# Differences of prepared weight blocks on GpSimd in place of VectorE, in an encoder kernel

## The chip, the cores and the metric

One core of a Trainium2 chip runs the whole program. The metric is the device time of one execution in microseconds (us); of several runs the median counts.

The engines go by their short names in the profile: PE is TensorE (matmuls; PEld is its loading of the stationary operand), DVE is VectorE, ACT is ScalarE, POOL is GpSimd, and SP is the engine whose queue issues most of the DMAs.

## The reference

Two layers of a bidirectional encoder on x of 256 tokens by 1024 features, in float32:

```python
for l in range(DEPTH):                                     # DEPTH = 2
    x = x + 0.5 * swiglu(rms_norm(x, ffn1_norm[l]), ffn1_w_gate[l], ffn1_w_up[l], ffn1_w_down[l])
    h = rms_norm(x, mix_norm[l])
    ...                                                    # two kinds of attention on h, gated and merged
    x = x + merged @ w_out[l]
    x = x + 0.5 * swiglu(rms_norm(x, ffn2_norm[l]), ffn2_w_gate[l], ffn2_w_up[l], ffn2_w_down[l])

def swiglu(x, w_gate, w_up, w_down):
    return (jax.nn.silu(x @ w_gate) * (x @ w_up)) @ w_down  # 1024 -> 2816 -> 1024
```

There are thus four feed-forward stages, and the change touches nothing else.

## The kernel before

**Split operands.** Every matmul is made three times with split operands: a value is taken apart into a rounded part (high, made by ScalarE at line 190) and the rest (low, made by VectorE at line 191 as value minus high), and the products high by high, high by low and low by high are added up (lines 174 to 176). So each tile of weights is loaded from memory into one of four `raw` buffers (128 x 1024 values, `RAW = 4`), then ScalarE writes `wh` and VectorE writes `wl`, each in a ring of six, and TensorE uses both. The raw buffer is free once `wl` is written.

**Gate and up.** A feed-forward stage works through 11 chunks of 256 hidden features. A chunk loads four tiles of gate and up weights and makes 48 matmuls of 128 x 512, 24 for each of the two tiles of tokens, into one of two PSUM banks `g`. `glu` then makes `hh` from a bank: ScalarE applies silu to the gate half (line 463), VectorE multiplies by the up half (line 464). When that is done, the bank is free for the chunk after. `send` passes `hh` to a DMA transpose (ScalarE line 332, SP line 335). `arrive`, a chunk or so later, puts the transposed result together in a buffer `a` (ScalarE line 344), makes four sums and differences of its 128 x 128 blocks (VectorE, line 351) and splits it into `hi` and `lo`.

**Down.** The down projection takes the hidden features in pairs of blocks. For a chunk marked F or G in `PLAN = "SFGFGGFGGSS"`, its 2 x 2 blocks of weights are multiplied with the 2 x 2 blocks of hidden values by seven products in place of eight. This needs differences of weight blocks, which `differences` makes: two of 128 x 512 into a tile `u`, two into a tile `v` that build on those of `u`. `u` and `v` are then split like weights. `u`, `v` and the buffer `a` of `arrive` share two buffers (the tag `sums`), so a `v` waits until the `a` of its chunk has been split.

**Preparation.** Of the eight such pairs in a stage, three have their differences made early, during gate and up, where `prepare` keeps the split parts (`uh`, `ul`, `vh`, `vl`) until the down projection. `PREP = {3: 1, 5: 3, 7: 6}` says at which gate-and-up chunk the pair of which chunk is prepared; the first stage of all has `PREP_FIRST = {5: 1, 7: 3, 8: 6}`. A preparation loads two rows of blocks into raw buffers, which it holds until the last difference that reads them. The other five pairs have theirs made in the down projection, by `sevens`.

**Order.** TensorE runs in the order of the code. A scheduler orders the instructions of the other engines by its own estimate of their times, and each engine then runs its queue strictly in that order.

Of the kernel before, what the change touches and what calls it, by code (L numbers as in the profile page):

```python
# [17 lines left out]
ALU = mybir.AluOpType  # L18
# [40 lines left out]
def hybrid_encoder(ctx, tc, x, w_gu1, w_d1, w_in, b_gate, qk_gain, rpb, sink, t5,  # L59
                   w_bna, w_bsw, w_out, w_gu2, w_d2, c_mask, c_band, out):  # L60
    nc = tc.nc
# [127 lines left out]
    def split_to(hi, lo, src):  # L189
        last_hi[0] = linked("act", lambda: nc.scalar.activation(hi, src, AF.Copy))  # L190
        linked("dve", lambda: nc.vector.tensor_tensor(lo, src, hi.bitcast(F32), ALU.subtract))  # L191
# [126 lines left out]
    def ffn(l, n, w_gu, w_d, after):  # L318
        with tc.tile_pool(name="ffn", bufs=1) as fp:
# [40 lines left out]
            stored = {}  # L360

            def block_row(k, c0=0, n=2):
                r = ring.tile([P, 2, 512], F32, name="raw", tag="raw", bufs=RAW)[:, :n, :]
                nc.sync.dma_start(r, w_d[l, k * P:(k + 1) * P, :n * 512].rearrange("p (h n) -> p h n", h=n))
                return r

            def differences(r0, r1, into):
                sub = lambda to, x, y: nc.vector.tensor_tensor(to, x, y, ALU.subtract)  # L368
                u = fp.tile([P, 2, 512], F32, name="u", tag="sums", bufs=2)
                sub(u[:, 0, :], r1[:, 1, :], r0[:, 1, :])  # L370
                sub(u[:, 1, :], r0[:, 1, :], r0[:, 0, :])
                us = into("u", u)
                v = fp.tile([P, 2, 512], F32, name="v", tag="sums", bufs=2)
                sub(v[:, 0, :], r1[:, 1, :], u[:, 1, :])
                sub(v[:, 1, :], r1[:, 0, :], v[:, 0, :])
                return us, into("v", v)

            def prepare(c):
                def into(name, r):
                    hl = [fp.tile([P, 2, 512], F32R, name=f"{name}{p}{c}", tag=f"{name}{p}{c}") for p in "hl"]  # L380
                    split_to(*hl, r)
                    return hl
                stored[c] = differences(block_row(2 * c), block_row(2 * c + 1), into)

            def sevens(c):
                r0 = block_row(2 * c, n=1 if c in stored else 2)
                r1 = block_row(2 * c + 1)
                place = ("xh0", "xl0", "xh1", "xl1")[(c - PLAN[:c].count("S")) % 4]
                both = act.tile([P, 2, 512], F32R, name="corner", tag=place)
                corner = [both[:, i, :] for i in range(2)]  # L390
                split_to(*corner, r0[:, 0, :])
                low = parts(r1)
                us, vs = stored.get(c) or differences(r0, r1, lambda name, r: parts(r))
                if on_way and c >= 5:
                    arrive()
                half = lambda pair, i: [p[:, i, :] for p in pair]
                return (("1", 0, corner), ("2", 1, half(low, 0)), ("3", 6, half(low, 1)), ("5", 3, half(us, 1)),
                        ("6", 4, half(vs, 0)), ("4", 2, half(vs, 1)), ("7", 5, half(us, 0)))
# [67 lines left out]
            for c in range(NFC):  # L466
                first = n == 0 and c == 0
                pair = [None]
                if first:
                    both, second = opening(w_gu, l, lambda ps: glu(0, ps, pair))  # L470
                elif n == 0 and c == 1:
                    pieces = second
                else:
                    pieces = columns(w_gu, l, c * 512, 512)
                if c >= 2:
                    arrive()
                prep = PREP if n else PREP_FIRST
                if c in prep:
                    prepare(prep[c])
                for t in range(T):  # L480
                    if not first:
                        glu(t, project(t, pieces, 512), pair)
                    elif t:
                        glu(t, both[t], pair)
                send(c, pair[0])
# [376 lines left out]
```

## Time and profile before

| | |
|---|---|
| median of three runs | 1064.51 us (1064.47 to 1069.99) |
| profiled execution | 1065.35 us; the span from first to last instruction is 1063.6 us |
| TensorE, VectorE, ScalarE, GpSimd busy | 1051.7, 879.6, 746.6, 117.7 us |
| granted TensorE clock | 1.00 of full speed over the span |
| DMA | 224.15 MB, the queue of SP busy 72.4% of 16 engines' span |

Rows of the timeline give the start in us from the span's start, the duration in us, the engine, the line, the operation, the tile written and those read, the shapes, and at the end, in brackets, how long the engine had been idle and what ended that. "Waits" give the waiting engine and its line, an arrow, who ended the wait, and then total us, times and longest us. TensorE's matmuls overlap: one of 128 x 512 shows about 0.39 us, and the next starts before it ends, so the step from start to start is what counts. Rows by source line give the shortest, median and longest duration in ns.

### The profile page before, as it was taken

How to read it: one execution, taken by the hardware profiler on the slowest of the kernel's cores; microseconds unless marked ns; L12 is line 12 of the kernel's file. 1: busy time of each engine (PE TensorE's matmuls, PEld its weight loads, DVE VectorE, ACT ScalarE, POOL GpSimd, SP SyncE). 2: the span in 40 equal slices, each digit the busy share in tenths (PEclk: the TensorE clock that was granted, in tenths of full speed). 3: DMA queues.
4: the chain of work that ended last, by engine and by line, in shares of the span. 5: the costliest groups of instructions: out<-in, count | busy, mean ns of one | idle time of the engine just before them, and what ended most of it. 6: DMA issues, size and time to landing. Idle time of an engine off the chain costs nothing.

```text
span 1063.6 us, 14462 instructions
## 1 busy us (share of the span) xinstructions
PE 1051.7 (99%) x4949; PEld 870.7 (82%) x4949; DVE 879.6 (83%) x1337; ACT 746.6 (70%) x1070; POOL 117.7 (11%) x118
## 2 busy tenths in 40 slices
PE   8999999999999999999999999999999999999998
PEld 6888787888888888888788888878888888878886
DVE  6678899889886858879977887998898866788797
ACT  6777775788773667786567886757887646678772
POOL 1000130243420000000000000004534100000000
PEclk9999999999999999999999999999999999999999
DMA  7989875765654589996758998757566546799862
GB/s 246 263 220 268 253 207 191 222 197 154 195 181 155 170 234 253 248 252 196 224 174 226 262 259 213 215 160 247 175 195 179 190 156 192 215 256 245 240 203 98
DMA packets 145291, 224.15 MB, mean 211 GB/s; under 512 B 54033, under 2 KB 60209, under 8 KB 145217
## 3 DMA queue, kind: packets, MB, share of 16 engines
q1 hardware_dynamic: 145024, 223.14, 72.4%
q8 instruction: 39, 0.64, 0.3%
q14 instruction: 36, 0.29, 0.1%
q0 software_dynamic: 192, 0.08, 0.1%
HBM read 210.59 MB, written 1.06 MB: 199 GB/s over the span
## 4 chain that ended last, share of the span: by engine, by line
PE 55%; DVE 16%; DMA 16%; ACT 7%; issue 4%; SPq 0%; ACTq 0%; DVEq 0%
PE g L174 12%; PE g L176 12%; PE g L175 12%; DMA raw<-in_w_gu 10%; DVE wl L191 8%; DMA raw<-in_w_d 4%; PE acc L174 3%; PE acc L176 3%; PE acc L175 3%; ACT a L344 3%; ACT wh L190 2%; ACT lo L332 2%; DVE v L368 2%; PE sc L585 1%; PE po L620 1%
## 5 line engine op out<-in xcount | busy, mean ns | idle before, releaser
L191 DVE TENSOR_TENSOR wl<-raw,wh 128x1024 fp32r<-128x1024 f32 x336 | 405.4, 1219 | 63.5 <-ACT wh L190 60.7
L190 ACT ACTIVATE wh<-raw 128x1024 fp32r<-128x1024 f32 x336 | 345.2, 1042 | 99.8 <-DMA raw<-in_w_gu 44.9
L174 PE MATMUL g<-wh,xh 128*128 128x512 f32 (+1 forms) x976 | 382.5, 392 | 0.8 <-DVE hh L464 0.3
L175 PE MATMUL g<-wl,xh 128*128 128x512 f32 (+1 forms) x976 | 377.5, 387 | 0.4 <-DVE wl L191 0.4
L176 PE MATMUL g<-wh,xl 128*128 128x512 f32 (+1 forms) x976 | 377.4, 387 | 0.0
L176 PEld LDWEIGHTS g<-wh,xl 128*128 128x128 f32 x976 | 183.4, 188 | 38.5 <-DVE xl L191 0.6
L174 PEld LDWEIGHTS g<-wh,xh 128*128 128x128 f32 x976 | 183.5, 188 | 38.2 <-DVE hh L464 4.8
L175 PEld LDWEIGHTS g<-wl,xh 128*128 128x128 f32 x976 | 183.6, 188 | 34.4 <-DVE wl L191 1.4
L175 PE MATMUL acc<-wl,hi 128*128 128x512 f32 x180 | 70.2, 390 | 0.9 <-DVE wl L191 0.9
L174 PE MATMUL acc<-wh,hi 128*128 128x512 f32 x180 | 70.7, 393 | 0.0
L176 PE MATMUL acc<-wh,lo 128*128 128x512 f32 x180 | 70.1, 390 | 0.0
L180 POOL TENSOR_TENSOR rs_y<-ms,mhalf 128x1 f32<-128x1 f32 x12 | 7.7, 645 | 547.0 <-DVE ms L228 538.3
L344 ACT ACTIVATE a<-hi 128x1024 uint16<-128x1024 uint16 x44 | 59.5, 1353 | 0.0
L332 ACT ACTIVATE lo<-hh 128x1024 uint16<-128x1024 uint16 x44 | 46.2, 1051 | 18.4 <-DVE hh L464 18.3
L464 DVE SCALAR_TENSOR_TENSOR hh<-g,rs_y,hh 128x256 f32<-128x256 f32 x88 | 42.1, 479 | 18.0 <-ACT hh L463 18.0
L351 DVE TENSOR_TENSOR a<-a 128x128 f32<-128x128 f32 x128 | 32.0, 287 | 28.9 <-ACT a L344 28.1
L463 ACT ACTIVATE hh<-g,rs_y 128x256 f32<-128x256 f32 x88 | 40.4, 459 | 19.4 <-PE g L176 19.0
L368 DVE TENSOR_TENSOR u<-raw 128x512 f32<-128x512 f32 x64 | 42.2, 690 | 13.1 <-DMA raw<-in_w_d 12.8
L191 DVE TENSOR_TENSOR lo<-a,hi 128x896 fp32r<-128x896 f32 (+1 forms) x44 | 43.0, 977 | 11.1 <-ACT hi L190 11.1
L598 POOL TENSOR_TENSOR S<-S,sm 128x512 f32<-128x512 f32 x32 | 37.2, 1161 | 65.5 <-DVE sm L597 38.2
L190 ACT ACTIVATE hi<-a 128x896 fp32r<-128x896 f32 (+1 forms) x44 | 37.7, 856 | 8.6 <-DVE a L351 8.0
L190 ACT ACTIVATE corner<-raw 128x512 fp32r<-128x512 f32 x32 | 20.0, 626 | 30.8 <-DMA raw<-in_w_d 27.6
(186 smaller groups left out, 1506.3 us busy)
## 6 DMA issues: line engine op xcount, KB each, us to landing
raw<-in_w_gu SPq DMA_DIRECT2D x176, 512.0 KB, 4.6
raw<-in_w_d SPq DMA_DIRECT2D x100, 512.0 KB, 4.4
raw<-in_w_in SPq DMA_DIRECT2D x64, 512.0 KB, 4.6
raw<-in_w_out SPq DMA_DIRECT2D x16, 512.0 KB, 3.5
bb<-in_b_gate SPq DMA_DIRECT2D x16, 256.0 KB, 3.5
raw<-in_w_bsw SPq DMA_DIRECT2D x8, 512.0 KB, 3.9
raw<-in_w_bna SPq DMA_DIRECT2D x8, 512.0 KB, 3.6
raw<-in_w_d SPq DMA_DIRECT2D x12, 256.0 KB, 2.6
```

Source lines behind the costliest of these rows:

```text
L174: nc.tensor.matmul(ps, xh, wh, start=first, stop=False)
L175: nc.tensor.matmul(ps, xh, wl, start=False, stop=False)
L176: nc.tensor.matmul(ps, xl, wh, start=False, stop=last)
L190: last_hi[0] = linked("act", lambda: nc.scalar.activation(hi, src, AF.Copy))
L191: linked("dve", lambda: nc.vector.tensor_tensor(lo, src, hi.bitcast(F32), ALU.subtract))
L332: apart[c] = nc.scalar.activation(z.rearrange("p (two n) -> p two n", two=2), hh.bitcast(U16).rearrange("p s (n two) -> p two (s n)", two= ...
L344: joined = nc.scalar.activation(a[:, :4, :].bitcast(U16).rearrange("p s (n two) -> p two (s n)", two=2), zT.rearrange("p (two s) n -> p tw ...
L351: nc.vector.tensor_tensor(a[:, to, :], a[:, x, :], a[:, y, :], op)
L368: sub = lambda to, x, y: nc.vector.tensor_tensor(to, x, y, ALU.subtract)
L463: linked("act", lambda: nc.scalar.activation(h, gate, AF.Silu, scale=rstd[t]))
L464: linked("dve", lambda: nc.vector.scalar_tensor_tensor(h, up, rstd[t], h, op0=ALU.mult, op1=ALU.mult))
L598: nc.gpsimd.tensor_tensor(S_, S_, sm.unsqueeze(2).to_broadcast([P, T, S]), ALU.mult)
```

## The change

`differences` gets the engine that subtracts as an argument. `prepare`, the caller in gate and up, passes GpSimd; `sevens`, the caller in the down projection, passes nothing and stays on VectorE.

```diff
-            def differences(r0, r1, into):
-                sub = lambda to, x, y: nc.vector.tensor_tensor(to, x, y, ALU.subtract)
+            def differences(r0, r1, into, engine=nc.vector):
+                sub = lambda to, x, y: engine.tensor_tensor(to, x, y, ALU.subtract)
                 u = fp.tile([P, 2, 512], F32, name="u", tag="sums", bufs=2)
                 sub(u[:, 0, :], r1[:, 1, :], r0[:, 1, :])
                 sub(u[:, 1, :], r0[:, 1, :], r0[:, 0, :])
...
-                stored[c] = differences(block_row(2 * c), block_row(2 * c + 1), into)
+                stored[c] = differences(block_row(2 * c), block_row(2 * c + 1), into, nc.gpsimd)
```

The scheduler's order moves with it. On VectorE, at the second preparation of a stage with `PREP` (here the second stage, chunk 5), this is the piece up to the product hh of that chunk's first tile of tokens:

```order
 L464 SCALAR_TENSOR_TENSOR hh<-g,rs_y,hh 128x2x128
-L368 TENSOR_TENSOR u<-raw 128x512 x2
-L351 TENSOR_TENSOR a<-a 128x128 x4
-L191 TENSOR_TENSOR wl<-raw,wh 128x1024
+L351 TENSOR_TENSOR a<-a 128x128 x4
+L191 TENSOR_TENSOR wl<-raw,wh 128x1024 x2
 L191 TENSOR_TENSOR ul_4203<-u,uh_4202 128x1024
-L191 TENSOR_TENSOR wl<-raw,wh 128x1024
 L191 TENSOR_TENSOR lo_4188<-a,hi_4187 128x896
 L464 SCALAR_TENSOR_TENSOR hh<-g,rs_y,hh 128x256
```

The two differences u are gone from VectorE, and the second split of weights now stands ahead of the split of u instead of behind it. The next piece is what follows there, up to the split of v:

```order
 L464 SCALAR_TENSOR_TENSOR hh<-g,rs_y,hh 128x256
-L191 TENSOR_TENSOR wl<-raw,wh 128x1024
-L368 TENSOR_TENSOR v<-raw,u 128x512
-L191 TENSOR_TENSOR wl<-raw,wh 128x1024
-L368 TENSOR_TENSOR v<-raw,v 128x512
-L191 TENSOR_TENSOR wl<-raw,wh 128x1024
+L191 TENSOR_TENSOR wl<-raw,wh 128x1024 x3
 L464 SCALAR_TENSOR_TENSOR hh<-g,rs_y,hh 128x2x128
 L191 TENSOR_TENSOR vl_4210<-v,vh_4209 128x1024
```

The two differences v no longer stand between the three splits of weights. On ScalarE, at the same preparation, between the copies of send and arrive (lo, a) and the chunk's silu (hh):

```order
 L332 ACTIVATE lo_4157<-hh 128x1024
 L344 ACTIVATE a<-hi_4066 128x2x512
-L190 ACTIVATE wh<-raw 128x1024
+L190 ACTIVATE wh<-raw 128x1024 x2
 L190 ACTIVATE uh_4202<-u 128x1024
-L190 ACTIVATE wh<-raw 128x1024
 L190 ACTIVATE hi_4187<-a 128x896
 L463 ACTIVATE hh<-g,rs_y 128x256
```

The high part of u moved behind the second split of weights. On GpSimd, the twelve differences of the first stage go between the load of the small bias table and the load of the vector that the bias of the second kind of attention is made in:

```order
 L496 DMA table<-in_t 8x32
+L368 TENSOR_TENSOR u<-raw 128x512 x2
+L368 TENSOR_TENSOR v<-raw,u 128x512
+L368 TENSOR_TENSOR v<-raw,v 128x512
+L368 TENSOR_TENSOR u<-raw 128x512 x2
+L368 TENSOR_TENSOR v<-raw,u 128x512
+L368 TENSOR_TENSOR v<-raw,v 128x512
+L368 TENSOR_TENSOR u<-raw 128x512 x2
+L368 TENSOR_TENSOR v<-raw,u 128x512
+L368 TENSOR_TENSOR v<-raw,v 128x512
 L495 DMA vec<-in_c_band 8x511
```

Nothing else in GpSimd's queue stands among them. SP's queue keeps its order but for the end of the first stage's gate and up, where a transpose moved by two loads.

## The prediction

> **What bounds the kernel now.** I read the busy shares first, then the waits of TensorE, then the instructions that the diff touches, then the timeline of one preparation.
>
> ```profile
> PE 1051.7 (99%) x4949; PEld 870.7 (82%) x4949; DVE 879.6 (83%) x1337; ACT 746.6 (70%) x1070; POOL 117.7 (11%) x118
> PE g L175 <- DVE wl L191: 0.4, 1, 0.4
> PE g L174 <- DVE hh L464: 0.3, 2, 0.2
> PEld g L174 <- DVE hh L464: 4.8, 11, 0.6
> PEld g L175 <- DVE wl L191: 1.4, 3, 0.9
> PEld acc L175 <- DVE wl L191: 1.3, 1, 1.3
> ```
>
> The first line is the busy time of the engines; the others are who waited for whom: total us, times, longest. TensorE (PE) is the bound. It waits on VectorE (DVE) for two things: the gated product hh, whose end frees a PSUM bank, and the low parts wl of the split weights. All of that is 4.8 + 1.4 + 1.3 = 7.5 us of idle weight loading at most, and 0.4 + 0.3 us of idle matmul in gate and up. That is the ceiling of any gain from relieving VectorE.
>
> What moves, and what GpSimd (POOL) needs for the same shape, stands in the rows by source line (ns min/median/max):
>
> ```profile
> L368 DVE TENSOR_TENSOR u<-raw x64: 676/685/959, 65.9 to 1039.9; 128x512 f32<-128x512 f32 x64
> L368 DVE TENSOR_TENSOR v<-raw,u x32: 677/685/694, 75.5 to 1040.6; 128x512 f32<-128x512 f32 x32
> L598 POOL TENSOR_TENSOR S<-S,sm x32: 1041/1042/1880, 226.8 to 831.1; 128x512 f32<-128x512 f32 x32
> L692 POOL TENSOR_TENSOR b<-t,mask x16: 1184/1194/2062, 240.5 to 818.6; 128x512 f32<-128x512 f32 x16
> L191 DVE TENSOR_TENSOR wl<-raw,wh x336: 683/1220/1987, 7.3 to 1048.4; 128x1024 fp32r<-128x1024 f32 x164, 128x512 fp32r<-128x512 f32 x4
> ```
>
> The maxima of the last three rows are worth following. The timeline of GpSimd (two rows) and VectorE (two rows) in the attention stage shows them:
>
> ```profile
> 247.06 1.04 POOL L598 TENSOR_TENSOR S<-S,sm 128x512 f32<-128x512 f32 x1 [2.22 <-PE g L176]
> 252.20 1.85 POOL L598 TENSOR_TENSOR S<-S,sm 128x512 f32<-128x512 f32 x1 [4.10 <-PE pt L606]
> 247.20 1.99 DVE L191 TENSOR_TENSOR wl<-raw,wh 128x1024 fp32r<-128x1024 f32 x1
> 251.95 1.20 DVE L191 TENSOR_TENSOR wl<-raw,wh 128x1024 fp32r<-128x1024 f32 x1
> ```
>
> At 247 GpSimd is first: the split that starts 0.14 us behind it takes 1.99 us in place of 1.22, 0.77 longer. At 251.95 VectorE is first, and GpSimd's operation takes 1.85 us in place of 1.04, 0.81 longer. So the two exclude each other, whoever comes first, when both read two tensors from SBUF; of GpSimd's 1.04 us, 0.14 + 0.77 = 0.91 are closed to VectorE. In gate and up nearly every VectorE instruction is of that kind.
>
> **The change part by part.** *Off VectorE:* 12 preparations (three in each of four feed-forward stages) of four differences, 48 x 0.685 = 32.9 us of its 879.6. *Onto GpSimd:* 48 operations. Their price on GpSimd is not in the trace; the two rows above bound it at 1.04 and 1.19 us. I take 1.04, since that operation, too, runs through plain rows of 512 and the other reads an overlapping pattern. *The lock:* if VectorE has work throughout, each costs it 0.91 and saves 0.685, that is 4 x 0.225 = 0.9 us more per preparation; if VectorE was idle, it saves up to 2.7. The answer lies in the windows, so here is the second preparation of the second feed-forward stage, VectorE first, then ScalarE (ACT), then the first matmul of the next chunk:
>
> ```profile
> 416.69 1.29 DVE L368 TENSOR_TENSOR u<-raw 128x512 f32<-128x512 f32 x2 [0.98 <-DMA raw<-in_w_d]
> 418.10 1.02 DVE L351 TENSOR_TENSOR a<-a 128x128 f32<-128x128 f32 x4
> 419.04 1.22 DVE L191 TENSOR_TENSOR wl<-raw,wh 128x1024 fp32r<-128x1024 f32 x1
> 420.17 1.22 DVE L191 TENSOR_TENSOR ul<-u,uh 128x1024 fp32r<-128x1024 f32 x1
> 421.31 1.22 DVE L191 TENSOR_TENSOR wl<-raw,wh 128x1024 fp32r<-128x1024 f32 x1
> 422.44 1.09 DVE L191 TENSOR_TENSOR lo<-a,hi 128x896 fp32r<-128x896 f32 x1
> 423.44 0.48 DVE L464 SCALAR_TENSOR_TENSOR hh<-g,rs_y,hh 128x256 f32<-128x256 f32 x1
> 424.33 1.23 DVE L191 TENSOR_TENSOR wl<-raw,wh 128x1024 fp32r<-128x1024 f32 x1 [0.41 <-ACT wh L190]
> 425.47 0.69 DVE L368 TENSOR_TENSOR v<-raw,u 128x512 f32<-128x512 f32 x1
> 426.19 1.23 DVE L191 TENSOR_TENSOR wl<-raw,wh 128x1024 fp32r<-128x1024 f32 x1
> 427.33 0.69 DVE L368 TENSOR_TENSOR v<-raw,v 128x512 f32<-128x512 f32 x1
> 427.99 1.23 DVE L191 TENSOR_TENSOR wl<-raw,wh 128x1024 fp32r<-128x1024 f32 x1
> 416.71 1.36 ACT L344 ACTIVATE a<-hi 128x1024 uint16<-128x1024 uint16 x1
> 418.87 1.04 ACT L190 ACTIVATE uh<-u 128x1024 fp32r<-128x1024 f32 x1
> 419.81 1.05 ACT L190 ACTIVATE wh<-raw 128x1024 fp32r<-128x1024 f32 x1
> 420.76 0.95 ACT L190 ACTIVATE hi<-a 128x896 fp32r<-128x896 f32 x1
> 424.44 0.39 PE L174 MATMUL g<-wh,xh 128*128 128x512 f32 x1
> ```
>
> *The u part.* Both u wait for their rows from memory until 416.69, on any engine. GpSimd then runs them 416.69 to 417.73 and 417.73 to 418.77. The four small a are ready when ScalarE's a ends, 416.71 + 1.36 = 418.07, and meet the second u's lock: they start at about 418.65 to 418.77 in place of 418.10, so +0.6. VectorE saved nothing by losing the u, as it then only waits. Behind them the order is a, wl, wl, ul, lo, hh without a gap, so hh is 0.6 late as well. ScalarE's order adds a second reason: uh now stands behind the second wh, so hi starts after uh. That wh ran at 419.81 without an idle row, so its weights had landed by then; hi starts between 420.76 and 0.94 later. At the late end lo starts at 423.1 in place of 422.44, +0.7, no more than the lock alone. I take 0.65.
>
> *The v part.* The first v waits for lo, in whose buffer it writes. It is therefore ready when VectorE reaches hh and is ahead of the next wl, where before it stood behind it. Lo ends 0.65 late at 424.2, v holds the lock until 425.1 or 425.2, and that wl starts there in place of 424.33: +0.8. It ends at 426.4, the second v goes next until 427.4, the second wl starts there in place of 426.19: +1.2. The third wl then starts at about 428.6 in place of 427.99: +0.6. So the weights' low parts come 0.6 to 1.2 late, and the raw buffers behind them are reloaded so much later.
>
> A preparation by itself thus costs 0.6 to 1.2 us of lateness, with GpSimd at 1.19 some 0.3 more; where VectorE would have been idle at every lock it costs 0. I take 1.0.
>
> *What covers it.* How long TensorE can do without hh is read at the start of the next chunk, here for the first and third preparation of the same stage (hh, then the matmul that needs its bank; in the third also the two matmuls ahead of it):
>
> ```profile
> 400.73 0.48 DVE L464 SCALAR_TENSOR_TENSOR hh<-g,rs_y,hh 128x256 f32<-128x256 f32 x1
> 402.68 0.39 PE L174 MATMUL g<-wh,xh 128*128 128x512 f32 x1
> 445.96 0.48 DVE L464 SCALAR_TENSOR_TENSOR hh<-g,rs_y,hh 128x256 f32<-128x256 f32 x1
> 445.78 0.39 PE L175 MATMUL g<-wl,xh 128*128 128x512 f32 x1
> 446.01 0.39 PE L176 MATMUL g<-wh,xl 128*128 128x512 f32 x1
> 446.49 0.50 PE L174 MATMUL g<-wh,xh 128*128 128x512 f32 x1
> ```
>
> The cover is 402.68 - 401.21 = 1.47 us in the first preparation and 424.44 - 423.92 = 0.52 in the second. In the third there is none: hh ends at 446.44 and the matmul starts at 446.49, 0.48 behind its predecessor, where the step ahead of it was 0.23. So the cover shrinks by about 1 us per preparation already: loads, ScalarE and VectorE around it are a chain that is slower than TensorE there, and lateness is carried on to the next one.
>
> *The sum.* First preparation: 1.0 late, covered by 1.47, carried on. Second: 0.65 of its own u part plus 1.0 carried, less 0.52, is 1.1 us of stall. Third: about 0.35 from the second's v part and 0.65 to 1.2 of its own, uncovered: 1.0 to 1.5, I take 1.3. That is 2.4 us per stage and 9.6 for four. The first stage prepares at chunks 5, 7 and 8 in place of 3, 5 and 7; I take it as like the others. With lateness 0.6 and nothing carried it is 0.1 + 0.6 = 0.7 per stage, 3 in all; with 1.5 and all carried 4.5 - 0.5 = 4 per stage, 16 in all.
>
> The profiled execution took 1065.35 us, 0.84 above the median of 1064.51. 1065.35 + 9.6 = 1074.95, and by the median 1074.1: I say 1074.
>
> *What costs nothing.* GpSimd has room: beside 117.7 us it gets 48 x 1.04 to 1.19, 50 to 57 us, none of it beside attention. The one queue piece behind the new operations, the bias vector at line 495, waits for ScalarE in any case and is first read in attention. SP issues in the same order in three stages; two of its loads per preparation now wait for GpSimd's last reading of a raw row instead of VectorE's, at 418.77 and 427.4 in place of 417.98 and 428.02: 0.8 late once, 0.6 early once, and in the sum with the lateness above.
>
> The Trainium skill has the exclusion as a rule ("SBUF — State Buffer", section "Who interferes with whom"): the shared port pair is an exclusive lock held for the whole instruction, and the other fully blocks. The 1.99 and 1.85 us above bear that out within 0.13 us; by the rule's letter each lock closes 1.04 and not 0.91, and as an estimate every preparation would be some 0.2 later, 2.4 us in all, which makes 1076.5.
>
> **The rivals.** *Not slower: the locks fall into idle time.* VectorE idles 0.98 ahead of u and 0.41 ahead of the first wl in the window, and it loses 2.74 us of work per preparation. If a preparation comes no more than 0.5 late and the chain makes that up before the next, only the uncovered third one stalls: 4 x 0 to 0.5 us on 1064.5, so 1064 to 1067. For it: the first preparation has 1.47 us of cover, and a chunk without one lies between. Against it: that chunk does not restore the cover today. It decides where lateness per preparation is under 0.5.
>
> *Faster: VectorE's relief counts.* Then the waits for hh and wl shrink: at most 7.5 us, 1057; half of it, 1061. Against it: VectorE's second half of every preparation is exchanged for a lock of at least the same length. The skill's "Perfetto Trace Analysis", section "Optimizing Scalar/DVE Operations", says that with a saturated VectorE moving work to GpSimd may make sense, and in the same place that the shared read port may make it useless; the 1.99 us row speaks for the second half.
>
> *Much slower: GpSimd lags.* If a difference takes 1.2 and waits out a split of 1.22 each time, the chain u, u, v, v takes 4 x 2.4 = 9.7 us beside a window of about 15; raw rows are held longer, and if that doubles the lateness, 2 x 9.6 = 19 us make 1084. Against it: at 247 the lock was GpSimd's as soon as it came free.
>
> **How the numbers follow.** Forecast 0.60 (1067 to 1081), not slower 0.27, faster 0.06, much slower 0.07. About 0.5%, 5.3 us, is what a measurement tells from no change here. Slower: 0.55 of the forecast and the much slower, 0.62. Same: the rest of the forecast, the not slower, half of the faster: 0.35. Faster: 0.03. The range from 1063 to 1081 leaves out the much slower and most of the faster.
>
> **What would show it.** GpSimd busy at 170 us or more, with differences of 1.04 to 1.2 and some near 1.9; splits near 1.9 in gate and up; VectorE's busy time down by clearly less than 32.9; waits of TensorE for hh at the second and third preparations, together near 10 us in place of 4.8. Wrong if hh still ends ahead of its matmul there, or if the waits for wl grow and those for hh do not.

## The result, and the profile after

The changed kernel took 1076.63 us (median of 6 runs, 1074.41 to 1079.14), the kernel before, beside it, 1068.67 (median of 6, 1064.47 to 1069.99). The ratio is 1.0084, 95% interval 1.0066 to 1.0101: slower, by 8 to 9 us. The median of 1064.51 that stood at the start was that of three runs, two of them at the low end of what later runs show. The profiled execution of the changed kernel took 1077.21 us, its span is 1075.4.

The rows below are the busy times on the page, then the waits of TensorE, then the rows by source line of the moved differences and of the split (ns min/median/max), and the group of all splits of weights (busy us, mean ns).

```profile
PE 1055.4 (98%) x4949; PEld 870.4 (81%) x4949; DVE 879.2 (82%) x1289; ACT 746.9 (69%) x1070; POOL 196.1 (18%) x166
PEld g L174 <- DVE hh L464: 16.0, 17, 2.3
PE g L174 <- DVE hh L464: 8.5, 8, 1.9
PEld g L175 <- DVE wl L191: 5.2, 10, 2.1
L368 POOL TENSOR_TENSOR u<-raw x24: 1288/1299/2280, 62.7 to 975.7; 128x512 f32<-128x512 f32 x24
L368 POOL TENSOR_TENSOR v<-raw,u x12: 1280/1287/1294, 75.0 to 983.4; 128x512 f32<-128x512 f32 x12
L368 POOL TENSOR_TENSOR v<-raw,v x12: 2149/2154/2162, 76.4 to 984.8; 128x512 f32<-128x512 f32 x12
L191 DVE TENSOR_TENSOR wl<-raw,wh x336: 680/1220/2367, 7.4 to 1060.3; 128x1024 fp32r<-128x1024 f32 x164, 128x512 fp32r<-128x512 f32 x4
L191 DVE TENSOR_TENSOR wl<-raw,wh 128x1024 fp32r<-128x1024 f32 x336 | 430.2, 1297 | 65.6 <-ACT wh L190 63.0
```

VectorE lost 48 instructions, 32.9 us of work, and is as busy as before: 879.2 us against 879.6. What was taken off came back mostly as longer splits, 430.2 us now; of before the same group's row is

```profile
L191 DVE TENSOR_TENSOR wl<-raw,wh 128x1024 fp32r<-128x1024 f32 x336 | 405.4, 1219 | 63.5 <-ACT wh L190 60.7
```

A difference takes GpSimd 1.29 us, and the second v of every preparation takes 2.15, since it waits for a split to end. TensorE's waits for hh went from 4.8 to 16.0 us.

The second preparation of the second feed-forward stage, to be read beside the window in the prediction: GpSimd, VectorE, ScalarE, then the next chunk's first matmul.

```profile
419.85 2.55 POOL L368 TENSOR_TENSOR u<-raw 128x512 f32<-128x512 f32 x2 [10.35 <-DMA raw<-in_w_d]
429.60 1.29 POOL L368 TENSOR_TENSOR v<-raw,u 128x512 f32<-128x512 f32 x1 [7.20 <-DVE lo L191]
430.97 2.15 POOL L368 TENSOR_TENSOR v<-raw,v 128x512 f32<-128x512 f32 x1
422.77 1.02 DVE L351 TENSOR_TENSOR a<-a 128x128 f32<-128x128 f32 x4 [2.40 <-ACT a L344]
426.09 1.23 DVE L191 TENSOR_TENSOR wl<-raw,wh 128x1024 fp32r<-128x1024 f32 x1 [1.16 <-ACT wh L190]
429.37 0.48 DVE L464 SCALAR_TENSOR_TENSOR hh<-g,rs_y,hh 128x256 f32<-128x256 f32 x1
429.87 5.46 DVE L191 TENSOR_TENSOR wl<-raw,wh 128x1024 fp32r<-128x1024 f32 x3
425.00 1.06 ACT L190 ACTIVATE wh<-raw 128x1024 fp32r<-128x1024 f32 x1 [1.36 <-DMA raw<-in_w_gu]
425.97 1.04 ACT L190 ACTIVATE uh<-u 128x1024 fp32r<-128x1024 f32 x1
429.90 0.50 PE L174 MATMUL g<-wh,xh 128*128 128x512 f32 x1 [1.11 <-DVE hh L464]
454.32 0.50 PE L174 MATMUL g<-wh,xh 128*128 128x512 f32 x1 [1.91 <-DVE hh L464]
```

Both u run from 419.85 to 422.40, for the most part while VectorE is idle (its hh before ends at 420.38): its four a wait 2.40 us for ScalarE and start at 422.77. No lock touches them. ScalarE waits 1.36 us for the weights of the second wh, and only then comes uh, then hi, lo and hh. Behind hh both v hold VectorE: three splits take 5.46 us, where three without a lock take 2 x 1.14 + 1.23 = 3.51. But VectorE's own two v, 0.69 us each, no longer stand between them: the last of the three ends 5.96 us behind the start of hh, against 5.78 in the window of before. TensorE waits 1.11 us for hh here and 1.91 at the third preparation.

So two things stood side by side: the lock, and an order on ScalarE that the scheduler chose along with it. The experiments take them apart.

### The profile page after: what moved, and what is told of

Same layout as the page of the kernel before. It is cut to its first block, busy times and chain, and to the rows that moved or that the text cites. A ratio compares the mean times of both kernels' runs of the same rounds, so it can differ in the third digit from the quotient of the medians.

```text
span 1075.4 us, 14504 instructions
## 1 busy us (share of the span) xinstructions
PE 1055.4 (98%) x4949; PEld 870.4 (81%) x4949; DVE 879.2 (82%) x1289; ACT 746.9 (69%) x1070; POOL 196.1 (18%) x166
## 4 chain that ended last, share of the span: by engine, by line
PE 54%; DVE 19%; DMA 13%; ACT 8%; issue 5%; POOL 1%; ACTq 0%; DVEq 0%; POOLq 0%
PE g L174 12%; PE g L176 12%; PE g L175 12%; DVE wl L191 10%; DMA raw<-in_w_gu 9%; DMA raw<-in_w_d 3%; ACT wh L190 3%; PE acc L174 3%; PE acc L176 3%; PE acc L175 3%; DVE lo L191 2%; ACT a L344 2%; ACT lo L332 1%; PE sc L585 1%; PE po L620 1%
## 5 line engine op out<-in xcount | busy, mean ns | idle before, releaser
L191 DVE TENSOR_TENSOR wl<-raw,wh 128x1024 fp32r<-128x1024 f32 x336 | 430.2, 1297 | 65.6 <-ACT wh L190 63.0
L368 POOL TENSOR_TENSOR u<-raw 128x512 f32<-128x512 f32 x24 | 34.9, 1474 | 186.4 <-DMA raw<-in_w_d 149.4
L190 ACT ACTIVATE corner<-raw 128x512 fp32r<-128x512 f32 x32 | 20.0, 625 | 32.9 <-DMA raw<-in_w_d 30.3
```

The lines of the kernel that those rows point to most:

```text
L368: sub = lambda to, x, y: engine.tensor_tensor(to, x, y, ALU.subtract)
```

## The experiments

The ratios are to the kernel before, run beside each of them. "Stalls" is worked out from the start times of the matmuls in each trace: by how much the steps of gate and up, behind the first chunk of a stage, exceed the usual step of 0.227 us, where it is over 0.1 us, summed over the second, third and fourth feed-forward stage. The first stage is kept apart, for a reason that the control shows.

| kernel | differences on GpSimd | uh behind the second wh | ratio, 95% interval | stalls, stages 2 to 4 | stage 1 |
|---|---|---|---|---|---|
| before | none | no | 1 | 2.5 us | 1.4 us |
| before again | none | no | 0.9998 (0.9979 to 1.0017) | 2.9 | 7.0 |
| uh late | none | yes | 1.0013 (0.9994 to 1.0032) | 4.6 | 4.1 |
| v only | v | no | 0.9992 (0.9978 to 1.0006) | 1.1 | 3.6 |
| uh first | u and v | no | 1.0004 (0.9989 to 1.0019) | 4.8 | 5.6 |
| u only | u | yes | 1.0026 (1.0006 to 1.0046) | 2.8 | 3.8 |
| v late | v | yes | 1.0060 (1.0040 to 1.0080) | 10.3 | 3.0 |
| changed again | u and v | yes | 1.0076 (1.0052 to 1.0101) | 9.3 | 4.8 |

### Order put back

```diff
     def split_to(hi, lo, src):
         last_hi[0] = linked("act", lambda: nc.scalar.activation(hi, src, AF.Copy))
+        if ahead[0] is not None:        # set to uh for the second wh of the next chunk
+            behind(last_hi[0], ahead[0])
+            ahead[0] = None
```

> The changed kernel with one order put back: ScalarE's split of u (uh) again stands ahead of the second weight split of the next chunk, as in the kernel before, in all preparations; VectorE's ul follows it. GpSimd still makes all 48 differences. Order theory (uh, and with it hi, lo and hh, are late because they stand behind a split whose weights land late): most of the 8.0 us comes back, ratio to before 0.998 to 1.003, waits for hh back near 5 us. Lock theory (GpSimd's differences themselves hold VectorE's splits up): nothing or little comes back, ratio 1.005 to 1.009, waits for hh still near 16 us.

1070.19 us, 1.0004. The loss is gone within what the runs can tell (1.6 us), with all 48 differences still on GpSimd and the locks still there: the group of splits takes 428.1 us, nearly as in the changed kernel. The stalls of its trace, 4.8 us, are half of the changed kernel's, though above the 2.5 to 2.9 of before. In the second to fourth stage no other order differs from the changed kernel's but VectorE's ul, which follows uh.

```profile
L200 DVE TENSOR_TENSOR wl<-raw,wh 128x1024 fp32r<-128x1024 f32 x336 | 428.1, 1289 | 59.4 <-ACT wh L196 56.8
PEld g L178 <- DVE hh L475: 8.0, 13, 1.5
```

The prediction's first reason, the lock, is therefore not enough for the loss. Is the order enough?

### Order alone

```diff
+        for i in ks:                    # in columns(): the next chunk's weights
+            made.append(load(...))
+            if i == 1 and waiting[0] is not None:   # waiting: the last uh
+                behind(waiting[0], last_hi[0])
```

> The kernel before, with all differences on VectorE, and the one order of the changed kernel: ScalarE's split of u (uh) behind the second weight split of the next chunk in every preparation. The order written by the scheduler follows it in a few more places (VectorE's ul behind the second wl, one transpose of SyncE behind a load of the down weights). Order theory: this alone costs what the change costs, +5 to +10 us, ratio 1.005 to 1.009, waits for hh from 4.8 to 10 or more. If the order only hurts together with GpSimd's locks: 0 to +3 us, ratio 1.000 to 1.003.

1072.06 us, 1.0013, not to be told from no change, and well under the changed kernel. The order alone shows in the trace as stalls of 0.63 to 0.80 us at four of six second and third preparations, 4.6 us in place of 2.5 to 2.9; it is a part of the loss, not the loss. But the scheduler moved more than uh here: at the second preparation, for one, the second v stands behind the third split of weights and ScalarE's vh behind a further wh, and SP's queue has a transpose behind a load. So the run doesn't show what the late uh alone would cost without GpSimd; it shows that a kernel with it need not lose 8 us.

### Only u, only v, and v with the late order

```diff
-                stored[c] = differences(block_row(2 * c), block_row(2 * c + 1), into)
+                stored[c] = differences(..., into, nc.vector, nc.gpsimd)   # u, v; u only: the other way round
```

"v late" takes this together with the edit of "order alone".

> Only the two differences v of each preparation on GpSimd, u on VectorE as before; ScalarE's uh stands ahead of the second weight split of the next chunk, as before. My prediction gave the v part 0.6 to 1.2 us per preparation, half and more of the sum: +4 to +6 us of 8, ratio 1.004 to 1.006. Order theory (the harm is in the u part, by uh behind a late split): 0.998 to 1.002.

> Only the two differences u of each preparation on GpSimd, v on VectorE as before; the scheduler's order then has uh behind the second weight split of the next chunk, as in the changed kernel. Order theory: the whole loss, ratio 1.005 to 1.010, though half of the locks are gone. By the steps of the prediction (0.65 us of lateness per preparation, cover of 1.47, 0.52 and 0): about 0.1 in the second and 0.65 in the third preparation, 3 us in all, ratio 1.003.

> Only the differences v on GpSimd, and uh behind the second weight split of the next chunk (the scheduler keeps that order in the first two preparations of the stages that prepare at chunks 3, 5 and 7, and of the first stage in places; in the last preparation of the first stage it differs). Each of the two alone measured nothing that can be told from no change (0.999 for v on GpSimd, 1.001 for uh behind). If costs add: ratio 1.000 to 1.002. If late order and GpSimd's v part meet (v waits for lo, which is late, and its lock then falls on splits that are already late): 1.004 to 1.008, most of the change's loss.

1066.79 us, 1073.20 and 1075.39. The v part by itself costs nothing, not the 4 to 6 us of my steps. Moving u, with the late order (and other moves of the scheduler, much as in "order alone"), costs 2.8 us on the ratio (0.6 to 4.9), and its stalls in the last three stages are those of the kernel before; where the 2.8 us fall isn't shown. But v on GpSimd with the late order costs 6.4 us and has the stalls of the changed kernel, where the two single effects add to 0.5 (0.0013 - 0.0008). The costs do not add. The pair of v only and v late is a clean one: on no engine's queue does anything differ but uh behind the second wh, and ul with it, and that is worth 0.0068, 7.3 us. Here are ScalarE, VectorE and GpSimd at the second preparation of the second stage, first with v only, then with v and the late order:

```profile
420.94 1.04 ACT L190 ACTIVATE uh<-u 128x1024 fp32r<-128x1024 f32 x1
422.21 1.06 ACT L190 ACTIVATE wh<-raw 128x1024 fp32r<-128x1024 f32 x1 [0.23 <-DMA raw<-in_w_gu]
423.18 0.94 ACT L190 ACTIVATE hi<-a 128x896 fp32r<-128x896 f32 x1
425.51 0.47 DVE L465 SCALAR_TENSOR_TENSOR hh<-g,rs_y,hh 128x256 f32<-128x256 f32 x1
425.91 2.19 DVE L191 TENSOR_TENSOR wl<-raw,wh 128x1024 fp32r<-128x1024 f32 x1
428.41 1.93 DVE L191 TENSOR_TENSOR wl<-raw,wh 128x1024 fp32r<-128x1024 f32 x1 [0.31 <-ACT wh L190]
425.73 1.29 POOL L374 TENSOR_TENSOR v<-raw,u 128x512 f32<-128x512 f32 x1 [18.59 <-DVE lo L191]
```

```profile
422.21 1.06 ACT L196 ACTIVATE wh<-raw 128x1024 fp32r<-128x1024 f32 x1 [1.83 <-DMA raw<-in_w_gu]
423.18 1.04 ACT L196 ACTIVATE uh<-u 128x1024 fp32r<-128x1024 f32 x1
424.12 0.94 ACT L196 ACTIVATE hi<-a 128x896 fp32r<-128x896 f32 x1
426.59 0.48 DVE L473 SCALAR_TENSOR_TENSOR hh<-g,rs_y,hh 128x256 f32<-128x256 f32 x1
426.98 5.55 DVE L197 TENSOR_TENSOR wl<-raw,wh 128x1024 fp32r<-128x1024 f32 x3
426.80 1.28 POOL L380 TENSOR_TENSOR v<-raw,u 128x512 f32<-128x512 f32 x1 [20.35 <-DVE lo L197]
```

The weights of the second wh let it start at 422.21 in both. Where uh stands ahead, it fills ScalarE's wait; where it stands behind, its 0.94 us come on top, and hi starts 0.94 later (424.12 against 423.18), hh 1.08 later. The v follow lo and so are later by the same. In the first case hh is early enough for its matmul, and VectorE still waits 0.31 us between locked splits; in the second it is late, and the splits run without a gap. The two traces do not run in step, though: the 41st matmul of the stage starts at 370.83 in the first and at 369.95 in the second. Measured from TensorE, the weights of that wh thus land 0.88 us later in the second (their load took 5.42 us from issue to landing against 4.77, and was issued 0.23 later), and hh is 1.08 + 0.88 = 1.96 late. In the second stage of these kernels that load takes 4.0 to 5.5 us to land; why, no run tells. A late uh costs the more, the later its neighbour's weights land.

With both, the second preparations of the last three stages stall TensorE by 0.95, 0.69 and 0.91 us and the third by 1.51, 1.53 and 1.65; with v only, by 0.3 at most; with the order alone, by 0.73, 0.80 and 0.70, then 0.63, 0.26 and 0.18. So at the second preparation the late order passes the cover by itself, and what the pair adds falls mostly on the third. The way there can be followed in the traces: SP's next loads wait for a raw buffer and go out as the first split behind hh ends. With v only that split ends at 425.91 + 2.19 = 428.10, with both at 426.98 + 2.19 = 429.17, and SP's rows are

```profile
428.13 2.61 SPq L142 DMA_DIRECT2D raw<-in_w_gu  x3
429.19 2.60 SPq L142 DMA_DIRECT2D raw<-in_w_gu  x3
```

With the order alone nothing locks that split; it takes 1.23 us. Measured from the 41st matmul, the weights of the third preparation's second wh land at 73.1 us with v only, at 74.6 with the order alone and at 76.1 with both, where TensorE itself is 0, 0.9 and 1.5 us behind. The waits for hh in the second stage's gate and up tell the same, before, order alone, v alone, both, changed:

```profile
PEld g L174 <- DVE hh L464: 1.0, 2, 0.5
```

```profile
PEld g L179 <- DVE hh L472: 1.9, 2, 1.0
```

```profile
PEld g L174 <- DVE hh L465: 0.2, 1, 0.2
```

```profile
PEld g L179 <- DVE hh L473: 4.0, 4, 1.8
```

```profile
PEld g L174 <- DVE hh L464: 5.7, 6, 2.3
```

### The lock without the relief

```diff
+                    made = nc.gpsimd.tensor_copy(gate1, x)     # x: u, then lo: sets the place
+                    for _ in range(2):
+                        more = nc.gpsimd.tensor_tensor(spare, xs[0][:, :512], xs[1][:, :512], ALU.subtract)
+                        ...
```

In the two siblings the last line writes zeros (three times as often, `memset`) or copies one row (`tensor_copy`). All three keep the order of before on VectorE, ScalarE, SyncE and TensorE.

> The kernel before, with VectorE still making all differences and the same order on VectorE, ScalarE, SyncE and TensorE, and beside it on GpSimd in each preparation four more differences of two 128x512 rows of the residual, two once u is there and two once lo is there, whose result nobody reads (it is written where vl is stored later). Lock theory: they cost VectorE what the real ones cost, 24 to 50 us of longer VectorE operations over the run, and without the 33 us of relief; so +4 to +16 us, ratio 1.004 to 1.015. Order theory: the order is that of before, so no change, ratio 0.998 to 1.003.

> As the run with four more differences per preparation on GpSimd, but with twelve writes of zeros to the same tile in their place: GpSimd is as busy in the same places and reads nothing from SBUF. Lock theory with the lock held by operations that read two inputs from SBUF: no change, 0.998 to 1.003. If GpSimd's being busy, or its writes, or the later start of vl is what costs: as much as the differences, 1.004 or more.

> As the run with four more differences per preparation on GpSimd, which cost 27 us, but with four copies of one 128x512 row in their place: one input from SBUF and not two. If the lock is there for every GpSimd operation that reads SBUF: +10 to +27 us, ratio 1.010 to 1.025. If it takes two inputs: 0.998 to 1.003, as the zeros.

1095.75 us, 1.0250 (1.0233 to 1.0267), for the differences; 1067.40, 0.9984 (0.9968 to 1.0000), for the zeros; 1074.65, 1.0053 (1.0033 to 1.0073), for the copies. The busy times of the first, and GpSimd's row of each:

```profile
PE 1061.1 (97%) x4949; PEld 869.0 (80%) x4949; DVE 920.3 (84%) x1337; ACT 747.8 (68%) x1070; POOL 195.6 (18%) x190
L388 POOL TENSOR_TENSOR vl<-x,x x48: 1278/1360/2167, 67.1 to 1000.3; 128x512 fp32r<-128x512 f32 x48
```

```profile
L389 POOL MEMSET vl<- x144: 517/527/534, 66.9 to 978.2; 128x512 f32 x144
```

```profile
L388 POOL CAST vl<-x x48: 612/617/1487, 67.4 to 982.1; 128x512 fp32r<-128x512 f32 x48
```

VectorE is 40.7 us busier for 48 differences, 0.85 us each, and the kernel 27 us slower, with no order changed and nobody waiting for the results. Zeros keep GpSimd just as busy and cost nothing. So the lock is real and comes with reading, and 48 added differences are far dearer than the change. That the relief of 32.9 us pays for the difference is likely but not shown: the added differences also stand elsewhere, those for u behind u, when VectorE is busy, where the changed kernel's u mostly falls into its idle time. Copies of one row do not go free either: 5.7 us, more than my second expectation and less than my first, with VectorE 9.1 us busier (888.7).

### Relief without the lock

```diff
+                    nc.gpsimd.tensor_copy(gate1, x[:, :1])     # in place of a difference
+                    made = nc.gpsimd.tensor_copy(gate1, y[:, :1])
+                    for _ in range(MANY):                      # MANY = 2
+                        more = nc.gpsimd.memset(to, 0.5)
+                        ...
```

> The kernel with uh put ahead again and without the locks: in place of each of the 48 differences GpSimd copies one column of each input (so that it waits for the same data) and then writes the 128x512 tile twice with a constant. The differences are left out of the computation. VectorE is relieved of 33 us and nothing of GpSimd's reads two tensors. Theory that the lock gives back just what the relief brings: VectorE's busy time near 847 us, and the time at most 7.5 us below before, likely 0 to -5, ratio 0.995 to 1.000. If the relief is worth nothing here in any case, since TensorE bounds: 0.998 to 1.002, and the waits for hh as in before.

This kernel leaves the differences out and writes a constant where they would stand; uh stands ahead again. 1075.41 us, 1.0047 (1.0030 to 1.0063), outside both expectations. VectorE is relieved: 850.4 us busy.

```profile
PE 1056.0 (98%) x4949; PEld 870.4 (81%) x4949; DVE 850.4 (79%) x1289; ACT 746.2 (69%) x1070; POOL 198.2 (18%) x310
SPq L146 <- POOL gate L385: 51.8, 18, 5.8
```

The run doesn't decide what it was made for. The scheduler gave it an order of its own, with transposes of SyncE behind further loads, and loads wait 51.8 us for GpSimd's small copies; its stalls fall on other chunks than those of the changed kernel. It shows only that 29 us less of VectorE buy nothing where the order and the loads around it are worse.

### The first preparation, and two controls

```diff
+                                        nc.gpsimd if c == (1, 3, 6)[0] else nc.vector)    # in prepare()
```

> Only the first preparation of each feed-forward stage on GpSimd, the other two on VectorE; in the first the scheduler's order has uh behind the second weight split. Cover as predicted (1.47 us ahead of the next matmul in the first preparation, what is left over carried to the second): 1.0 late per stage, carried 0.5, so 0 to +2 us in all, ratio 1.000 to 1.002. If the first preparation costs as much as the others: a third of the loss, +2.5 us, ratio 1.0025.

> The kernel before once more, as a run of its own: how far the ratio of equal kernels lies from 1 (0.998 to 1.002), and how much one profile differs from another in the waits for hh (4.8 us in the first) and in the stalls around the chunks at 113 us.

> The changed kernel once more, on the chip of the runs beside it, since the runs that undo one part are compared with it: 1.0084 within 0.002, waits for hh near 16 us, and stalls at the second and third preparation. If the ratio is below 1.005 here, part of the first figure was the chip's or the session's.

The first preparation alone on GpSimd, with the late order there: 1068.20 us, 0.9980 (0.9962 to 0.9998). It costs nothing, but it doesn't try the cover: in the last three stages hh ends 1.48, 1.48 and 1.44 us ahead of its matmul, as in the kernel before, since the weights of the second wh land in time and no wait stands ahead of uh. In the changed kernel ScalarE waits 1.43 us for them there. Here are hh and its matmul in the second stage, in this kernel and in the changed one:

```profile
403.24 0.48 DVE L465 SCALAR_TENSOR_TENSOR hh<-g,rs_y,hh 128x256 f32<-128x256 f32 x1
405.20 0.39 PE L174 MATMUL g<-wh,xh 128*128 128x512 f32 x1
405.75 0.48 DVE L464 SCALAR_TENSOR_TENSOR hh<-g,rs_y,hh 128x256 f32<-128x256 f32 x1
406.30 0.49 PE L174 MATMUL g<-wh,xh 128*128 128x512 f32 x1
```

In the changed kernel hh has 0.07 us left, 1.4 less, and TensorE still doesn't wait for it: here the cover is used up and holds. Nor is the first preparation alone a gain, for the run with zeros reads 0.9984 with the order and the work of the kernel before.

The changed kernel again: 1.0076, 13.1 us of waits for hh, and stalls at the same preparations (1.48 and 1.49 us in the second stage). The kernel before again: 0.9998. But its profile differs from the first:

```profile
PEld g L174 <- DVE hh L464: 9.6, 11, 1.9
PEld g L175 <- DVE wl L191: 3.1, 5, 0.9
```

Its first stage alone stalls 7.0 us, where the first profile has 1.4 and the changed kernel 6.7 and 4.8. The first stage's stalls thus differ as much from run to run as with the change, and the profile that the prediction was read from was a lucky one. In the other three stages equal kernels agree within 0.8 us (2.5 and 2.9; 10.1 and 9.3).

## Why the prediction was right, and where not

**The size.** The forecast was 9.6 us, 2.4 per stage; measured are 8 to 9. The 1074 is under the 1076.63 although the loss was set too high, since its base, 1064.51, was 4 us under the 1068.67 measured beside the change. In the three stages that can be told, stalls rose from 2.5 and 2.9 to 10.1 and 9.3, by 7.0 us in the mean, 2.3 per stage, though unevenly: the fourth stage has less than half of what the second has. The first stage, "I take it as like the others", isn't borne out: no difference shows there over the noise of one run, so one of the four terms stands on nothing, and that the sum of all four came so near is in part luck.

**The places.** The second preparation was to stall 1.1 us and the third 1.3. The two profiles of the changed kernel have, for the second stage, 1.28 and 2.07, then 1.48 and 1.49; for the third 1.34 and 1.36, then 0.71 and 1.35. In the fourth only the third preparation stalls much, 0.81 and 1.30. The first preparation was to be covered, and is: hh keeps 0.07 to 1.37 us there in the last three stages of the two profiles.

**The u part: near in size, by luck, and wrong in its cause.** The step that failed is "they start at about 418.65 to 418.77 in place of 418.10", the lock on the a. VectorE was idle there. Of ScalarE's order I wrote "+0.7, no more than the lock alone" and dropped it, since the larger of two covers the other. With no lock, it was the only one, and worth 0.94 on ScalarE, 1.08 at hh, beside the 0.65 that I took. It could have been read: the trace of before has the weights of that second wh landing at 419.52, so moved up to 418.87 it had to wait 0.65, and all of uh stood behind that wait.

**The v part.** "The weights' low parts come 0.6 to 1.2 late" had 0.65 of the u part in it, so 0.15, 0.55 and nothing for the v part. Counted from the start of hh, the three splits of the window end 0.5, 0.85 and 0.2 us later than before: each 0.2 to 0.35 more than forecast, since a difference takes 1.29, and GpSimd's second v waits out a split in all twelve preparations. That wait is a piece of the rival "GpSimd lags". By itself the v part costs nothing (0.9992).

**Cover and carry** is the step that carried the forecast, and the runs bear its form out: the first preparation's lateness is covered, the second's stalls TensorE, and the third stalls more. Moving uh alone back takes the loss away in two clean pairs (1.0084 to 1.0004, 1.0060 to 0.9992). How lateness is carried on I had left open: the loads behind wait for the end of the first locked split, as the rows of SP show. The share of that was not tried apart, nor was the late uh without GpSimd and without other moves.

**GpSimd's price** was bounded at 1.04 to 1.19 us and is 1.29. The bounds came from operations with other operands, and I took them for ends. The Trainium skill ("GPSIMD Engine Reference", section "Elementwise — side-by-side cycle accounting") has 2.6 cycles per element with two inputs; as an estimate at the 1.2 GHz it uses there, 512 of them are 1.11 us before any dispatch, which spoke against the 1.04 that I took, and the rows, at 1.29, agree.

**The relief.** "VectorE's busy time down by clearly less than 32.9": down 0.4. The rival "not slower" was true of a change that keeps the order (1.0004 and 0.9992); it would have come with uh put back. The rival "faster" has no run for it: none of the kernels beats the one before by more than equal kernels differ.

**The Trainium skill's rule** ("SBUF — State Buffer", section "Who interferes with whom"), an exclusive lock for the whole instruction, holds within 0.2 us: a locked split takes about 2.31 us, 2.37 at most, so 1.09 to 1.15 more than 1.22, beside a difference of 1.29. The estimate of 1076.5 by its letter came nearer than mine, but not for its reason: with the order put back the same locks cost nothing that can be told. The same section lets VectorE's two-input operations meet only GpSimd operations that read SBUF; the zeros (0.9984) and the copies (1.0053) agree.

## What to carry to other kernels

An instruction moved to another engine can change the order of a third one that the diff does not name: compare the orders, and price each moved row by what stands behind it when its own input is late. Two latenesses on one chain need not add: what stays below the cover isn't seen in the time, and what passes it can delay the loads behind, so test them together and apart before blaming either, and see what else the scheduler moved in each test. Read a base profile twice before a stage of it is used as a term: here one stage differed by 5.6 us between equal kernels. And set two traces in step on the bounding engine before times of one are compared with times of the other.

## What the runs showed of the hardware

A 128x512 GpSimd operation takes 0.53 us when it reads nothing, 0.62 with one full input, 1.04 with a second one spread from a column, and 1.29 with two full inputs from SBUF. It excludes VectorE's two-input splits already with one input: the 0.62 us copy takes up to 1.49 when it has to wait for a split, and 48 copies cost 5.7 us, 48 differences 27, 144 writes nothing. 48 differences on GpSimd cost between nothing that can be told, with VectorE relieved and uh ahead, and 27 us, without the relief and behind other work of VectorE's; the share of the relief and that of the place were not tried apart.
